# Turning the gated rows of both SwiGLU layers by transposing DMAs in 16-bit halves, in place of TensorE transposes

## The chip, the core and the metric

The kernel runs on one core of a Trainium2 chip. The core has TensorE (PE: matmuls, and in the profile PEld for the loads of the stationary operand), VectorE (DVE), ScalarE (ACT), GpSimd (POOL) and SyncE (SP), which here only issues DMAs. Each engine runs its own instructions in order and they meet at semaphores. SBUF is the memory on the chip (128 partitions), PSUM the eight banks that TensorE writes into, and 16 DMA engines move data. The metric is the device time of one execution in microseconds. Differences are told as time, and as a ratio where two kernels are compared.

## The reference

One decoder layer on 256 tokens of width 2048, all in float32:

```python
h = x
h = h + 0.5 * swiglu(rmsnorm(h, g_ffn1), w1_gate, w1_up, w1_down)      # f1
z = rmsnorm(h, g_mix) @ w_in
y = concat(rmsnorm(spatial_gating(...)), rmsnorm(window_attention_sinks(...)))
h = h + y @ w_out
h = h + cross_attention(rmsnorm(h, g_x), rmsnorm(mem, g_mem), w_xq, w_xkv, w_xo)
h = h + 0.5 * swiglu(rmsnorm(h, g_ffn2), w2_gate, w2_up, w2_down)      # f2
return rmsnorm(h, g_final)

def swiglu(x, w_gate, w_up, w_down):       # w_gate, w_up: 2048 x 5632, w_down: 5632 x 2048
    return (silu(x @ w_gate) * (x @ w_up)) @ w_down
```

The change touches the product silu(gate) * up of both SwiGLUs: a matrix of 256 tokens x 5632 columns that the next matmul contracts over its 5632 columns.

## The kernel before

**Products.** Every float32 operand is split into a high part that TensorE's fast 32-bit format (fp32r) holds exactly and a low part, the rest; a product takes three matmuls (high x high, low x high, high x low). `split` (L145 to L147) makes the two: ScalarE casts the high part (L146), VectorE subtracts it from the source for the low part (L147). Weights come as chunks of 1 MB, a tile of 128 x 4 x 512, and `load` issues their DMA on SP (L317 and L340) and splits them. Three raw chunks fit (tag raw, 3 buffers), and two of the split ones (tags wh and wl).

**Chunk kinds.** A chunk stands for a 2x2 block product. An N or C chunk takes 24 matmuls of 128x128 by 512 columns (four products of two terms); an S chunk takes 21, a seven-product form, and needs sums of weight blocks: VectorE makes them (tile t: L319, L322, L323), and they are split too (th and tl). The sums have one buffer each, so one S chunk's sums must be used up before the next one's take their place. An S chunk saves TensorE three matmuls and costs VectorE more.

**The gate/up stage of a SwiGLU.** `ffn` runs 11 units (index c, 0 to 10), each of eight chunks, for 512 columns of gate and the same 512 of up. Units 2 to 9 have four S chunks, the others three, and the first unit of f1 has none. When a unit's products are complete, `seven_early` and `seven_late` (L560 to L571) put them together from PSUM on VectorE, `gated` applies Silu on ScalarE (L671) and multiplies on VectorE (L675 in f1, L677 in f2), once for each half of the tokens (tb, 0 and 1). The result is two tiles of 128 tokens x 512 columns (`rows_`; in the profile f1gp and f1gz, f2gp and f2gz; f1sg in f1's first unit).

**The turn.** The down stage contracts over columns, so columns must lie on partitions. `rows_done(c, rows_)` does it: it takes an SBUF tile `a` (m4, 128 x 1024), and queues a generator `work` as side work. For each q (0 and 1) it calls `transposed` (L230), which does four 128x128 transposes on TensorE into one PSUM bank, two blocks of columns by two halves of the tokens, in the order that the kind of the down chunk wants (`laid`). ScalarE copies the bank to `a` (L665). `acts[2 * c + q]` is then set, and later `inner` fills the forms that the down stage multiplies.

**What sets the order.** TensorE's instructions run in program order. The other engines' order, SP's included, is laid out by a planner when the kernel is built: it simulates the program with its own estimates of durations, and takes what is ready by priority, earlier in the program first. `turn` keeps one chunk's matmuls pending: it writes the loads and splits of a chunk into the program, then the matmuls of the chunk before with its follow-up work (`post`, at high priority), and then those entries of the list `later` whose count has come to 0; each turn takes one off the counts. Side work is taken up during the matmuls, a step after every six (`side_step`), and a generator's `yield 5` asks for five steps of pause, `yield 2` for two. Thus the transposes of a unit's rows stand among the matmuls of the next unit's second and third chunks, or for the last unit among those of the first down chunks.

**Buffers.** Tag s2 has six buffers of 128 x 512 float32; it holds the parts of a unit while they are put together, the gated rows among them, and small intermediates. Tag tr has four PSUM banks, three of which the seven-product form uses.

Of the kernel before, what the change touches and what calls it, by code (L numbers as in the profile page):

```python
# [7 lines left out]

F32 = mybir.dt.float32
F32R = mybir.dt.float32r  # L10
AF = mybir.ActivationFunctionType
ALU = mybir.AluOpType
AX = mybir.AxisListType

P = 128
T = 256
TB = 2
# [15 lines left out]
def layer_kernel(  # L33
# [22 lines left out]
    nc = tc.nc  # L56
# [13 lines left out]
    def nm(s):  # L70
        uid[0] += 1
        return f"{s}_{uid[0]}"

    def m4(s):
        return mid.tile([P, 1024], F32, tag="m4", name=nm(s))

    def s2(s):
        return tmp.tile([P, 512], F32, tag="s2", name=nm(s))

    def bank(s):  # L80
        return trp.tile([P, 512], F32, tag="tr", name=nm(s))
# [8 lines left out]
    def silu_table():  # L90
        t = tiny.tile([P, 1], F32, tag="warmed", name=nm("warmed"))
        return nc.scalar.activation(t, ones[:, :1], AF.Silu)

# [24 lines left out]
    h = const.tile([P, TB, D], F32, name="h")  # L118
# [15 lines left out]
    def square_into(parts_ap, src, width):  # L134
        junk = s2("junk")
        nc.scalar.activation(junk[:, :width], src, AF.Square, accum_out=parts_ap)

    def split_scaled(hi, lo, src, g):

        nc.scalar.activation(hi, src, AF.Copy, scale=g)  # L140
        nc.vector.scalar_tensor_tensor(
# [27 lines left out]
    def form(s):  # L169
        return [fp.tile([P, 4, P], F32R, tag=t, name=nm(s + t)) for t in ("fh", "fl")]  # L170

    class Pair:
        def __init__(self, s, kind, base=None):
            self.kind = kind
            self.base = base or form(s)
            if kind in "SD":
                self.sums = form(s)
                if kind == "D":
                    self.more = [
                        const.tile([P, 2, P], F32R, tag="more" + t, name=nm(s + "more")) for t in "hl"  # L180
                    ]
# [40 lines left out]
    def laid(kind, k, tb):  # L222
        return BASE[kind].index(f"A{tb + 1}{k + 1}")

    def transposed(s, kind, src):

        ps = bank(s).rearrange("p (k t) -> p k t", k=4)
        for k in range(2):
            for tb in range(TB):
                nc.tensor.transpose(ps[:, laid(kind, k, tb), :], src(tb, k), ident)  # L230
        return ps

    def row_tile(kind, v, k):

        return v[:, k::2, :] if kind == "C" else v[:, 2 * k:2 * k + 2, :]

    def pair_from_rows(s, kind, src, gcol):
# [4 lines left out]
        for k in range(2):  # L242
# [4 lines left out]
            else:  # L247
                nc.scalar.activation(row_tile(kind, raw, k), row_tile(kind, ps, k), AF.Copy, scale=g)
        if kind != "N":
# [60 lines left out]
    def load(s, w, kind, pieces, between):  # L310

        raw = stream.tile([P, 4, 512], F32, tag="raw", name=nm(s + "w"), bufs=3)
        wh = stream.tile([P, 4, 512], F32R, tag="wh", name=nm(s + "wh"))
        wl = stream.tile([P, 4, 512], F32R, tag="wl", name=nm(s + "wl"))
        b = {name: (wh[:, i, :], wl[:, i, :]) for name, i in SLOT.items()}
        if kind == "S":
# [9 lines left out]
            for i, names in enumerate((("T1", "T3"), ("T2", "T4"))):  # L326
                th, tl = [
                    stream.tile([P, 2, 512], F32R, tag=f"{n}{i}", name=nm(s + n), bufs=1)
                    for n in ("th", "tl")
# [93 lines left out]
    def side_add(gen):  # L423
        side.append([now[0], gen])
# [33 lines left out]
    later = []  # L458
# [55 lines left out]
    def narrow_unit(s, w, pairs, late, beside):  # L514

        ps = []
        for c in range(2):
            raw = stream.tile([P, 8, 256], F32, tag="raw", name=nm(s + "w"), bufs=3)
            wh = stream.tile([P, 8, 256], F32R, tag="wh", name=nm(s + "wh"))
            wl = stream.tile([P, 8, 256], F32R, tag="wl", name=nm(s + "wl"))  # L520
# [33 lines left out]
    KINDS_D = "NNSNSNSN" + "NSNSNSN" + "NNSNSNN"  # L554
# [41 lines left out]
    def adds(s, c, j0, on_block=None):  # L596
# [10 lines left out]
        def early(u):  # L607
            p1, v, z = s2(s + "p1"), s2(s + "v"), s2(s + "z")
            nc.scalar.activation(p1, u["P1"], AF.Copy, scale=c)
            nc.vector.scalar_tensor_tensor(  # L610
# [40 lines left out]
    def ffn(s, get, rs, wgu, wd, on_block, first=None, on_token_block=None):  # L651
        acts = [None] * 22
        pairs = [None] * 22

        def rows_done(c, rows_):
            a = m4(s + "a").rearrange("p (q k t) -> p q k t", q=2, k=4)

            def work():
                for q in range(2):
                    yield 5 if q == 0 else 2  # L660
                    ps = transposed(
                        s + "a", KINDS_D[2 * c + q],
                        lambda tb, k: rows_[tb][:, (2 * q + k) * P:(2 * q + k + 1) * P],
                    )
                    nc.scalar.copy(a[:, q], ps)  # L665
                    acts[2 * c + q] = a[:, q]

            side_add(work())

        def gated(up, sg, r, tb):  # L670
            nc.scalar.activation(  # L671
                sg[1], sg[0], AF.Silu, scale=1.0 if r is None else r[:, tb:tb + 1]
            )
# [13 lines left out]
        def gu_unit(c):  # L687
            got = {}

            def late(u):  # L690
                r = rs()
                c22 = s2(s + "u")
                at = {(0, 0): got["p1"], (1, 1): c22, (0, 1): got["v"], (1, 0): got["z"]}
                seven_late(u, got, lambda tb, j: at[tb, j])
                gated(at[0, 1], (at[0, 0], at[0, 0]), r, 0)
                gated(c22, (at[1, 0], at[1, 0]), r, 1)
                rows_done(c, (at[0, 0], at[1, 0]))

            kinds = MORE if 2 <= c <= 9 else FEWER
            order = range(8)  # L700
            if c == (first is not None):
                order = ORDER[first is None]
            u = Unit(s + "g", "".join(kinds[j] for j in order))
            for i in range(8):
                push(
                    u, i, wgu[order[i], c], lambda j=order[i]: get(j),
                    lambda i=i: (
                        i == u.kinds.rindex("S") and seven_early(u, got), i == 7 and late(u)
                    ),
                    beside=lambda i: (  # L710
                        first[2](8 + i) if first is not None and c == 1
                        else rs() if (c, i) == (0, 5) else inner(i - 5) if c == 10 and i >= 5 else None
                    ),
                )

        def plain_gu_unit(c):
            pairs_, before, prep, rs0 = first
            u = Unit(s + "g", "N" * 8, alone=(7,))
            u.gate_first = True

            def late():
                r = rs0()
                sg = [s2(s + "sg") for _ in range(TB)]
                for tb, (g, up) in enumerate((("P2", "Q3"), ("Q4", "R"))):
                    gated(u[up], (u[g], sg[tb]), r, tb)
                rows_done(c, sg)

            pieces = {0: (1, 0, 3, 2), 1: (1, 3, 0, 2)}
            for i in range(8):
                push(  # L730
                    u, i, wgu[i, c], lambda i=i: have(pairs_, i), late if i == 7 else None,
                    pieces=pieces.get(i), beside=prep, before=before,
                )
# [747 lines left out]
```

## Time and profile before

| | |
|---|---|
| median of 3 runs | 2049.84 us (2049.66 to 2049.85) |
| span of the profiled execution (first to last instruction) | 2047.2 us |
| its own time, beside the span | not listed apart; the runs' median lies 2.6 us above the span |
| TensorE busy | 2034.8 us (99%) |
| VectorE busy | 1859.5 us (91%) |
| ScalarE busy | 1225.4 us (60%) |
| DMA engines | 402.21 MB, SP's queue 53.0% of 16 engines' span |
| TensorE clock granted | 0.999 of full speed |

Times are from one execution. A row of a group gives the line, engine, operation, what is written <- what is read with the shapes, how often, and durations; a row of the timeline gives the start and the length in microseconds, and in brackets how long the engine was idle before it and what ended that. Matmuls overlap, so the starts of neighbours tell what one costs, not its length. A wait row names who waited and for whom, with the total, the number and the longest.

### The profile page before, as it was taken

The page shows a single profiled execution, that of the slowest core. Times are in us where ns is not written, and L with a number is a line of the kernel's source. Part 1 is how long each engine was busy: PE and PEld are TensorE (multiplying, and loading weights), DVE is VectorE, ACT ScalarE, POOL GpSimd, SP SyncE. Part 2 cuts the span into 40 slices and gives each one's busy share as a digit, 9 for nine tenths or more (in the row PEclk, how much of TensorE's full clock was granted, in tenths as well). Part 3 has the DMA queues.
Part 4 walks back from the last instruction along what each step waited for, and adds up shares of the span by engine and source line. Part 5 has one row for each costly group of instructions (what it writes and reads, how often), then busy time and mean ns, then how long its engine had stood idle before and what let it go on. Part 6 is the DMA issues. An engine that isn't in the chain of part 4 may idle for free.

```text
span 2047.2 us, 24505 instructions
## 1 busy us (share of the span) xinstructions
PE 2034.8 (99%) x9411; PEld 1690.0 (83%) x9411; DVE 1859.5 (91%) x1998; ACT 1225.4 (60%) x1344; POOL 36.6 (2%) x57
## 2 busy tenths in 40 slices
PE   9999999999999999999999999999999999999998
PEld 7888888888888888888888888888888888888886
DVE  6999999999998978988988977899999999999988
ACT  7755555565555766655556665675555556565554
POOL 0000000000000110100000000000000000000000
PEclk9999999999999999999999999999999999999999
DMA  8555555555555565545545544455455555555563
GB/s 312 182 207 204 206 206 185 205 209 192 203 204 203 188 241 178 195 162 185 202 169 186 204 150 155 171 195 214 185 206 202 205 193 206 202 203 209 185 224 126
DMA packets 60421, 402.21 MB, mean 196 GB/s; under 512 B 6912, under 2 KB 8976, under 8 KB 13200
## 3 DMA queue, kind: packets, MB, share of 16 engines
q1 hardware_dynamic: 57856, 393.50, 53.0%
q0 software_dynamic: 2016, 6.30, 0.9%
q8 instruction: 74, 1.21, 0.2%
q10 hardware_dynamic: 432, 0.84, 0.1%
q14 instruction: 43, 0.35, 0.1%
HBM read 398.52 MB, written 2.10 MB: 196 GB/s over the span
## 4 chain that ended last, share of the span: by engine, by line
PE 97%; DVE 1%; ACT 1%; issue 0%; DMA 0%; POOL 0%; POOLq 0%; DVEq 0%; SPq 0%
PE f1gQ L410 16%; PE f2gQ L410 15%; PE f2dQ L410 6%; PE f1dQ L410 6%; PE f1gP L410 6%; PE f2gP L410 6%; PE xqQ L410 3%; PE f2dP L410 3%; PE f1dP L410 3%; PE woQ L410 2%; PE xoQ L410 2%; PE f2dR L410 2%; PE f1dR L410 2%; PE vQ L410 2%; PE mv0Q L410 2%; PE mv1Q L410 2%
## 5 line engine op out<-in xcount | busy, mean ns | idle before, releaser
L147 DVE TENSOR_TENSOR f1gwl<-f1gw,f1gwh 128x1536 fp32r<-128x1536 f32 (+2 forms) x94 | 181.7, 1935 | 19.8 <-ACT f1gwh L146 16.0
L146 ACT CAST f2gwh<-f2gw 128x1536 fp32r<-128x1536 f32 (+1 forms) x88 | 150.7, 1712 | 69.0 <-PE f2gQ L410 45.5
L146 ACT CAST f1gwh<-f1gw 128x1536 fp32r<-128x1536 f32 (+2 forms) x94 | 153.0, 1629 | 59.9 <-PE f1gQ L410 39.0
L147 DVE TENSOR_TENSOR f2gwl<-f2gw,f2gwh 128x1536 fp32r<-128x1536 f32 (+1 forms) x88 | 179.4, 2039 | 9.5 <-ACT f2gwh L146 7.8
L146 ACT CAST f2gth<-f2gt 128x1024 fp32r<-128x1024 f32 x82 | 84.9, 1050 | 75.9 <-DVE f2gt L319 28.8
L146 ACT CAST f1gth<-f1gt 128x1024 fp32r<-128x1024 f32 x76 | 79.0, 1051 | 76.1 <-DVE f1gt L319 30.1
L410 PE MATMUL f2gQ<-f2gwh,n4fh 128*128 128x512 f32 x317 | 124.5, 393 | 0.0
L410 PE MATMUL f2gQ<-f2gwh,n4fl 128*128 128x512 f32 x317 | 123.4, 389 | 0.0
L146 ACT CAST f2dwh<-f2dw 128x2048 fp32r<-128x2048 f32 (+1 forms) x44 | 77.3, 1757 | 61.6 <-PE f2dQ L410 39.6
L410 PE MATMUL f1gQ<-f1gwh,n1fh 128*128 128x512 f32 x286 | 112.4, 393 | 0.0
L410 PE MATMUL f1gQ<-f1gwh,n1fl 128*128 128x512 f32 x286 | 111.3, 389 | 0.0
L146 ACT CAST f1dwh<-f1dw 128x2048 fp32r<-128x2048 f32 (+1 forms) x44 | 77.3, 1758 | 56.6 <-PE f1dQ L410 38.1
L147 DVE TENSOR_TENSOR f2gtl<-f2gt,f2gth 128x1024 fp32r<-128x1024 f32 x82 | 99.6, 1220 | 8.9 <-ACT f2gth L146 8.4
L147 DVE TENSOR_TENSOR f1dwl<-f1dw,f1dwh 128x2048 fp32r<-128x2048 f32 (+1 forms) x44 | 92.1, 2093 | 12.6 <-ACT f1dwh L146 12.5
L147 DVE TENSOR_TENSOR f2dwl<-f2dw,f2dwh 128x2048 fp32r<-128x2048 f32 (+1 forms) x44 | 92.1, 2094 | 11.5 <-ACT f2dwh L146 11.3
L147 DVE TENSOR_TENSOR f1gtl<-f1gt,f1gth 128x1024 fp32r<-128x1024 f32 x76 | 92.4, 1220 | 7.7 <-ACT f1gth L146 7.2
L410 PE MATMUL f2gQ<-f2gwl,n4fh 128*128 128x512 f32 x317 | 97.6, 392 | 0.0
L410 PE MATMUL f1gQ<-f1gwl,n1fh 128*128 128x512 f32 x286 | 88.0, 393 | 0.0
L410 PEld LDWEIGHTS f2gQ<-f2gwh,n4fh 128*128 128x128 f32 x317 | 59.5, 188 | 12.3 <-DVE f2gv L569 0.4
L410 PEld LDWEIGHTS f2gQ<-f2gwh,n4fl 128*128 128x128 f32 x317 | 59.5, 188 | 11.9
L410 PE MATMUL f2gP<-f2gwh,n4fh 128*128 128x512 f32 x176 | 68.8, 391 | 0.0
L410 PEld LDWEIGHTS f2gQ<-f2gwl,n4fh 128*128 128x128 f32 x317 | 58.8, 188 | 12.0
(828 smaller groups left out, 6045.8 us busy)
## 6 DMA issues: line engine op xcount, KB each, us to landing
f2gw<-in_w_gu SPq DMA_DIRECT2D x88, 1024.0 KB, 4.8
f1gw<-in_w_gu SPq DMA_DIRECT2D x86, 1024.0 KB, 4.9
f1dw<-in_w_down SPq DMA_DIRECT2D x44, 1024.0 KB, 4.8
f2dw<-in_w_down SPq DMA_DIRECT2D x44, 1024.0 KB, 4.8
wow<-in_w_out SPq DMA_DIRECT2D x16, 1024.0 KB, 4.8
xqw<-in_w_xq SPq DMA_DIRECT2D x16, 1024.0 KB, 4.8
xow<-in_w_xo SPq DMA_DIRECT2D x16, 1024.0 KB, 4.8
qw<-in_w_in SPq DMA_DIRECT2D x8, 1024.0 KB, 4.8
```

Of the source, the lines that this page charges most:

```text
L146: nc.scalar.copy(hi, src)
L147: nc.vector.tensor_tensor(lo, src, hi.bitcast(F32), ALU.subtract)
L410: nc.tensor.matmul(self.banks[name], x, y, start=name not in self.begun, stop=self.left[name] == 0)
```

## The change

`rows_done` no longer uses TensorE, nor PSUM. A DMA transposes 16-bit elements, so the 32-bit rows are taken as pairs of 16-bit words:

- `turned`, in the turn in which the rows are gated: for each half of the tokens ScalarE copies the row tile (128 tokens x 512 float32, seen as 1024 words of 16 bits) into an s2 tile `w`, the 512 low halves first and the 512 high halves behind them. Then a transposing DMA on SP's queue turns `w` into another s2 tile `t`: eight blocks of 128x128 words, four of the low halves and four of the high ones, each with columns on partitions.
- `joined`, two turns later: for each q and each half of the tokens a ScalarE copy takes two blocks of low and of high halves from `t` and writes them interleaved into `a`, so that 32-bit numbers stand there again, at the places that `laid` gives. Then `acts` is set as before.

Both go through the list `later`, not through the side work. Per unit that is two parting copies of 128x1024 words, two transposing DMAs of 256 KB, and four joining copies of 128x512 words, in place of eight transposes and two copies of 128x512 from PSUM.

```diff
         def rows_done(c, rows_):
-            a = m4(s + "a").rearrange("p (q k t) -> p q k t", q=2, k=4)
-
-            def work():
+            a = m4(s + "a")
+            words = a.bitcast(U16).rearrange("p (q i t h) -> p q i t h", q=2, i=4, h=2)
+            halves_ = []
+
+            def turned():
+                for tb in range(TB):
+                    w = s2(s + "w").bitcast(U16)
+                    nc.scalar.copy(
+                        w.rearrange("p (h c) -> p h c", h=2),
+                        rows_[tb].bitcast(U16).rearrange("p (c h) -> p h c", h=2),
+                    )
+                    t = s2(s + "t").bitcast(U16)
+                    nc.sync.dma_start_transpose(t.rearrange("p (b r) -> p b r", b=8), w)
+                    halves_.append(t.rearrange("p (h b t) -> p b t h", h=2, b=4))
+
+            def joined():
                 for q in range(2):
-                    yield 5 if q == 0 else 2
-                    ps = transposed(
-                        s + "a", KINDS_D[2 * c + q],
-                        lambda tb, k: rows_[tb][:, (2 * q + k) * P:(2 * q + k + 1) * P],
+                    kind = KINDS_D[2 * c + q]
+                    for tb in range(TB):
+                        i, j = laid(kind, 0, tb), laid(kind, 1, tb)
+                        nc.scalar.copy(
+                            words[:, q, i:j + 1:j - i], halves_[tb][:, 2 * q:2 * q + 2]
+                        )
+                    acts[2 * c + q] = a[:, q * 512:(q + 1) * 512].rearrange(
+                        "p (k t) -> p k t", k=4
                     )
-                    nc.scalar.copy(a[:, q], ps)
-                    acts[2 * c + q] = a[:, q]
-
-            side_add(work())
+
+            later.append((0, turned))
+            later.append((2, joined))
```

`U16` is the 16-bit unsigned type.

More of the change, by code (lines that the diff above doesn't have):

```diff
@@ L10 @@
 F32R = mybir.dt.float32r
+U16 = mybir.dt.uint16
 AF = mybir.ActivationFunctionType
```

## The prediction

> **What bounds the kernel now.** I read the page first (busy times, the chain that ended last), then what TensorE waited for, then the stretch of one gate/up unit in order of time.
>
> ```profile
> span 2047.2 us, 24505 instructions
> PE 2034.8 (99%) x9411; PEld 1690.0 (83%) x9411; DVE 1859.5 (91%) x1998; ACT 1225.4 (60%) x1344; POOL 36.6 (2%) x57
> PE 97%; DVE 1%; ACT 1%; issue 0%; DMA 0%; POOL 0%; POOLq 0%; DVEq 0%; SPq 0%
> ...
> PE xoQ L410 <- ACT n4r L248: 1.2, 1, 1.2
> ```
>
> TensorE is the chain: 97% of it, and the longest of its waits is 1.2 us, once. Whatever leaves TensorE's in-order queue shortens the span, as long as the engines that feed it keep up. The page alone doesn't say whether they do; the stretches of one unit each do (columns: length, then busy us of PE, PEld, DVE, ACT, POOL, granted clock, DMA share, GB/s):
>
> ```profile
> 231.45:273.23 41.78, 41.78 (x192) 34.58 (x190) 40.05 (x38) 24.13 (x22) 0.00 (x0) 1.00 0.55 202
> 1566.66:1608.43 41.77, 41.77 (x192) 34.57 (x190) 40.15 (x38) 24.05 (x22) 0.00 (x0) 1.00 0.54 202
> 52.00:95.00 43.00, 43.00 (x207) 35.57 (x206) 42.81 (x54) 33.16 (x45) 0.00 (x0) 1.00 0.52 186
> ```
>
> In a unit with four S chunks TensorE needs all of 41.77 us and VectorE 40.05 to 40.15 of them; in FFN 1's second unit VectorE is busy 42.81 of 43.00. VectorE is a second bound about 1.6 us behind the first. ScalarE has 17.6 us to spare in a unit, and the DMA engines are half idle.
>
> **What is removed.** The transposes at L230, four in a group, and the two ScalarE copies behind them. The same eight weight matmuls with a group among them and without one (TensorE in order of time; start, length):
>
> ```profile
> 147.07 0.62 PE L410 MATMUL f1gP<-f1gwl,n1fh 128*128 128x512 f32 x2
> 147.53 0.27 PE L230 MATMUL f1a<-ident,f1gp 128*128 128x128 f32 x1
> ...
> 147.89 1.64 PE L410 MATMUL f1gQ<-f1gwl,n1fh 128*128 128x512 f32 x6
> 149.36 0.39 PE L410 MATMUL f1gP<-f1gwh,n1fh 128*128 128x512 f32 x1
> ...
> 158.27 0.61 PE L410 MATMUL f1gP<-f1gwl,n1fh 128*128 128x512 f32 x2
> 158.72 1.52 PE L410 MATMUL f1gQ<-f1gwl,n1fh 128*128 128x512 f32 x6
> 160.08 0.39 PE L410 MATMUL f1gP<-f1gwh,n1fh 128*128 128x512 f32 x1
> ```
>
> 149.36 - 147.07 = 2.29 us against 160.08 - 158.27 = 1.81 us: a group costs 0.48 us, not the 4 x 0.27 that its rows show, because matmuls overlap. The copies tell how many groups there are:
>
> ```profile
> L665 ACT COPY f1a<-f1a x22: 572/584/590, 64.6 to 485.6; 128x512 f32<-128x512 f32 x22
> L665 ACT COPY f2a<-f2a x22: 577/587/590, 1398.1 to 1820.8; 128x512 f32<-128x512 f32 x22
> ```
>
> 44 groups x 0.48 = **21.1 us off TensorE**, 0.96 in each of 22 units. That is the most this change can bring: nothing else is taken from the chain. ScalarE loses 2 x 0.58 = 1.2 us per unit.
>
> **What is added on ScalarE.** Per unit two copies that part the halves (128x1024, 16 bit) and four that join them (128x512). No row has a 16-bit operand; the nearest are the casts of as many elements:
>
> ```profile
> L146 ACT CAST f1gth<-f1gt x76: 1040/1052/1078, 53.0 to 457.6; 128x1024 fp32r<-128x1024 f32 x76
> L146 ACT CAST f1afh<-f1a x22: 610/618/632, 393.6 to 630.0; 128x512 fp32r<-128x512 f32 x22
> ```
>
> 2 x 1.05 + 4 x 0.62 = 4.6 us. From below, half of that if a 16-bit element took half the time; from above, double if a stride of two halved the rate. I take 4.6, since time here goes with the number of elements. Net 3.4 us per unit, 75 us in all, against 17.6 idle per unit: no bound by its sum. What counts is where they stand, since ScalarE runs in order and its casts feed VectorE. The places, in one unit of FFN 1 (ScalarE, VectorE, SP's issues, then TensorE):
>
> ```profile
> 270.73 1.05 ACT L146 CAST f1gth<-f1gt 128x1024 fp32r<-128x1024 f32 x1 [2.87 <-DVE f1gt L319]
> 272.66 1.91 ACT L146 CAST f1gwh<-f1gw 128x2048 fp32r<-128x2048 f32 x1 [0.87 <-PE f1gQ L410]
> 274.47 0.58 ACT L665 COPY f1a<-f1a 128x512 f32<-128x512 f32 x1
> 274.95 1.06 ACT L146 CAST f1gth<-f1gt 128x1024 fp32r<-128x1024 f32 x1
> 276.71 0.59 ACT L665 COPY f1a<-f1a 128x512 f32<-128x512 f32 x1 [0.70 <-PE f1a L230]
> 277.22 1.49 ACT L146 CAST f1gwh<-f1gw 128x1536 fp32r<-128x1536 f32 x1
> 284.71 1.91 ACT L146 CAST f1gwh<-f1gw 128x2048 fp32r<-128x2048 f32 x1
> ...
> 268.80 0.68 DVE L675 TENSOR_TENSOR f1gz<-f1u,f1gz 128x512 f32<-128x512 f32 x1
> 272.81 1.22 DVE L147 TENSOR_TENSOR f1gtl<-f1gt,f1gth 128x1024 fp32r<-128x1024 f32 x1
> 277.16 1.22 DVE L147 TENSOR_TENSOR f1gtl<-f1gt,f1gth 128x1024 fp32r<-128x1024 f32 x1
> 278.41 1.23 DVE L319 TENSOR_TENSOR f1gt<-f1gw 128x1024 f32<-128x1024 f32 x1
> 279.55 1.75 DVE L147 TENSOR_TENSOR f1gwl<-f1gw,f1gwh 128x1536 fp32r<-128x1536 f32 x1
> 284.85 1.23 DVE L147 TENSOR_TENSOR f1gtl<-f1gt,f1gth 128x1024 fp32r<-128x1024 f32 x1 [1.20 <-ACT f1gth L146]
> ...
> 268.31 0.33 SPq L317 DMA_DIRECT2D f1gw<-in_w_gu  x1
> 274.69 0.33 SPq L340 DMA_DIRECT2D f1gw<-in_w_gu  x1
> ...
> 279.05 1.07 PE L410 MATMUL f1gQ<-f1gtl,n1fh 128*128 128x512 f32 x4
> ```
>
> The second gated row is done at 269.48 and the first 0.6 earlier; ScalarE is idle from about 267.9 to 270.73. The parting copies take 268.9 to 271.0, push the cast at 270.73 by 0.3, and its reader on VectorE (272.81) has 1.0 to spare: nothing. Without that idle stretch they would cost 2.1 us of ScalarE ahead of a cast. The four joining copies fall where the two old ones stood, around 274.5 to 279, and are 2.5 - 1.2 = 1.3 us longer. The tight place is the cast at 274.95: its low half ends at 278.4, and TensorE reads the last of those four operands from about 279.5, 1.1 us later, and 0.96 less than that once the transposes are gone. Between 0 (they fill the idle time, and the cast goes ahead) and 1.3 us per unit (all of it ahead of a cast) I take 0.2, near the low end, since the first joining copy replaces an equal old one: 22 x 0.2 = **+4.4 us**.
>
> **What is added on SP and the DMA engines.** 44 transfers of 256 KB from SBUF to SBUF. No row transposes in a DMA; by size the nearest are (KB each, median us to landing):
>
> ```profile
> f1gw<-in_w_gu SPq DMA_DIRECT2D x86, 1024.0 KB, 4.9
> mTr<-in_memT POOLq DMA_DIRECT2D x16, 128.0 KB, 3.3
> n0r<-in_xT SPq DMA_DIRECT2D x7, 256.0 KB, 7.2
> out<-hg SPq DMA_DIRECT2D x1, 256.0 KB, 3.9
> sm<-in_small ACTq DMA_DIRECT2D x1, 52.0 KB, 2.5
> ```
>
> So 2.5 us (the smallest transfer) to 7.2 (the same size, queued among other loads). I take 4 to 5: 3.9 for the size, plus part of the load that SP issued at 268.31 and that moves until about 273. Issued at about 270.0 and 271.3, the pair lands by about 276. As bytes they are 11.5 MB beside 402 MB on engines that are busy 55% of the time: nothing. On SP a transfer waits for its parting copy and the next weight load waits behind it; that load is issued at 274.69, so the pair may hold the queue for 3 us before anything shifts, and its tile is first read at 284.71, 5 us after it lands. Were that cover gone, each us of delay would pass to TensorE. Lifetimes: the six s2 buffers hold the two rows and four more while the pair is under way, and two were free; the PSUM bank becomes free, which nothing waits for.
>
> **VectorE as the next bound.** TensorE now needs 41.77 - 0.96 = 40.81 us a unit, VectorE 40.05 to 40.15: only 0.7 us may stay idle, where 1.7 are idle today. A part is waiting for buffers that TensorE frees and shrinks by itself. The 1.20 at 284.85 is another kind: VectorE waits for a cast of what it has itself just made. At worst it stays whole and a unit takes 40.05 + 1.20 = 41.25; at best it goes, 40.81. I take the middle, 0.22 lost in each of 17 such units (eight in each FFN, and the second of FFN 1): **+3.7 us**.
>
> **The sum.** -21.1 + 4.4 + 3.7 = -13.0 us on a span of 2047.2. The median of the runs, 2049.84, lies 2.6 above the span, and I leave that as it is: **2036.8 us**. My own bounds for the forecast are 2028.7 (all 21.1) and 2041.
>
> **Rivals.** (1) *VectorE takes over*: the 17 full units keep 41.77 us because VectorE can't lose its idle time, and only the other five gain 0.96: 2049.8 - 4.8 = 2045. For it: 42.81 of 43.00. Against: TensorE never waits for VectorE today. Chance 0.20.
>
> (2) *Slower: ScalarE stands at the joining copies.* They are in order ahead of the cast at 277.22, whose reader on VectorE starts at 279.55. The cast must start by 278.06, three joining copies (1.85 us) before it, so the second transfer must land by 276.2, 4.9 us after its issue; from 5.6 on VectorE's spare 0.7 us is used up too, and from 6.6 the gain of 0.96 is gone. At 7.2 us (the row of that size) ScalarE starts the cast at 280.3, VectorE waits until 281.8, 2.25 us late, 1.55 beyond its spare: 42.36 us a unit, 22 x 0.6 = +13, 2063. For it: ScalarE's place in the order is laid out by a planner's estimate of the landing, and the true one is unknown. Against: loads four times the size land in 4.9. Chance 0.25.
>
> (3) *The turning goes block by block*, each of a transfer's eight 128x128 blocks paying a small transfer's landing: 8 x 2.5 = 20 us, 40 for the pair, so that ScalarE stands some 33 us in each unit: 22 x 33 = +726, about 2775. For it: nothing in this trace; against: a plain 1 MB load lands in 4.9 as one stream. Chance 0.07. The Trainium skill, "VectorE: DVE Perf Modes", section "The three transpose paths", speaks for it: it gives 1309 ns for one 128x128 bf16 block by DMA against 390 on TensorE. By that figure a transfer would be an estimated 10.5 us and the time an estimated 2,400; this trace has TensorE's side far lower (0.48 us for a group of four, in 32 bits), so the page's own comparison would be worse still for DMA. "DMA: Bandwidth & Descriptors", section "Latency and other measured facts", has 261 GB/s for such transfers, which would be an estimated 1 us each and agrees with the forecast; no run here shows either yet.
>
> **Chances and range.** Forecast 0.48, rivals 0.20, 0.25, 0.07. A difference under 0.2%, 4.1 us, can't be told from none: rival 1 straddles that edge (a little over half of it faster), and a small part of rival 2 lies within it. Faster 0.59, same 0.12, slower 0.29. The range runs from 2028 to 2063, which leaves out rival 3 and the worse half of rival 2.
>
> **What would show it.** Right: no L230 row on f1a and f2a, units of 40.8 to 41.1 us, the transposing DMAs landing in under 5 us, VectorE over 97% busy in a unit. Rival 1: units of 41.7 with TensorE waiting for low halves. Rival 2: ScalarE idle at the joining copies, put down to the transposing DMA, and TensorE waiting behind it. Rival 3: those DMAs landing in 10 us or more.

## The result, and the profile after

The changed kernel takes 2054.82 us (median; 2053.67 to 2056.67) beside 2049.76 us for the kernel before on the same chip: a ratio of 1.0027 (95% interval 1.0017 to 1.0036), 5.1 us slower, just past the 0.2% that can be told from no change. The forecast was 2036.8, 13.0 us faster. So the sign was wrong, though the time lies in the stated range, whose upper end came from rival 2 with a transfer of 7.2 us.

The page of the changed kernel (span, busy times, the chain that ended last by engine):

```profile
span 2051.8 us, 24290 instructions
...
PE 2021.7 (99%) x9235; PEld 1672.0 (81%) x9235; DVE 1859.9 (91%) x1998; ACT 1293.0 (63%) x1432; POOL 34.4 (2%) x57
...
PE 85%; DVE 5%; ACT 5%; DMA 3%; issue 2%; SPq 0%; POOL 0%; POOLq 0%; DVEq 0%; ACTq 0%
```

The 9411 - 9235 = 176 transposes are gone. But TensorE is 85% of the chain where it was 97%: ScalarE, VectorE and the DMA are on it now. TensorE's two longest entries in the view of waits (total us, times, longest), and ScalarE's for the transposing DMA, are new:

```profile
PE f1gQ L411 <- ACT f1gth L147: 8.7, 8, 2.4
PE f1gQ L411 <- DVE f1gtl L148: 6.9, 8, 0.9
...
ACT f1a L677 <- DMA f1t<-f1w: 20.1, 9, 3.8
ACT f2a L677 <- DMA f2t<-f2w: 10.2, 10, 1.2
```

(In this kernel the casts are at L147, the low halves at L148, the parting copies at L664, the transposing DMAs at L669, the joining copies at L677.) TensorE's two waits are in FFN 1, though ScalarE stands for the DMA in both FFNs. Where the time went is told by one VectorE row that each unit but FFN 1's first has once, `f1u` or `f2u`: from its first start to its last lie nine units of FFN 1 and ten of FFN 2. Before, then after:

```profile
L568 DVE TENSOR_TENSOR f1u<-f1gQ,f1gz x10: 680/684/686, 95.2 to 472.7; 128x512 f32<-128x512 f32 x10
L568 DVE TENSOR_TENSOR f2u<-f2gQ,f2gz x11: 684/684/686, 1388.5 to 1807.9; 128x512 f32<-128x512 f32 x11
```

```profile
L569 DVE TENSOR_TENSOR f1u<-f1gQ,f1gz x10: 681/683/685, 96.8 to 485.8; 128x512 f32<-128x512 f32 x10
L569 DVE TENSOR_TENSOR f2u<-f2gQ,f2gz x11: 683/684/686, 1400.8 to 1813.2; 128x512 f32<-128x512 f32 x11
```

FFN 1 takes 389.0 us between these starts where it took 377.5 (+11.5, and 1.6 more ahead of the first). FFN 2 takes 412.4 where it took 419.4 (-7.0). What lies between and behind them is 1.5 shorter. Together +4.6, which is 2051.8 - 2047.2. So the same change lost in one FFN and won in the other. One full unit of each, in the windows view (columns as in the prediction):

```profile
271.13:314.33 43.20, 41.38 (x181) 33.63 (x181) 40.13 (x39) 27.16 (x25) 0.00 (x0) 1.00 0.62 207
1607.41:1648.38 40.97, 40.97 (x182) 33.71 (x181) 40.16 (x38) 27.42 (x25) 0.00 (x0) 1.00 0.62 218
```

Both were 41.77. FFN 2 has nearly the forecast's best unit (40.81), with TensorE busy throughout. In FFN 1 TensorE is idle 1.8 of 43.20 us. The place, in order of time (start, length; ScalarE first, then VectorE, SP, TensorE):

```profile
275.59 1.04 ACT L664 COPY f1w<-f1gp 128x1024 uint16<-128x1024 uint16 x1
276.53 1.05 ACT L664 COPY f1w<-f1gz 128x1024 uint16<-128x1024 uint16 x1
279.92 0.68 ACT L677 COPY f1a<-f1t 128x512 uint16<-128x512 uint16 x1 [2.34 <-DMA f1t<-f1w]
280.50 1.05 ACT L147 CAST f1gth<-f1gt 128x1024 fp32r<-128x1024 f32 x1
281.46 1.85 ACT L677 COPY f1a<-f1t 128x512 uint16<-128x512 uint16 x3
283.22 1.90 ACT L147 CAST f1gwh<-f1gw 128x2048 fp32r<-128x2048 f32 x1
285.03 1.03 ACT L147 CAST f1gth<-f1gt 128x1024 fp32r<-128x1024 f32 x1
...
278.06 1.22 DVE L320 TENSOR_TENSOR f1gt<-f1gw 128x1024 f32<-128x1024 f32 x1
282.73 0.69 DVE L324 TENSOR_TENSOR f1gt<-f1gt,f1gw 128x512 f32<-128x512 f32 x1
285.15 2.29 DVE L148 TENSOR_TENSOR f1gwl<-f1gw,f1gwh 128x2048 fp32r<-128x2048 f32 x1 [1.73 <-ACT f1gwh L147]
...
276.66 2.62 SPq L669 DMA_TRANSPOSE f1t<-f1w  x2
...
286.11 0.50 PE L411 MATMUL f1gQ<-f1gth,n1fh 128*128 128x512 f32 x1 [0.95 <-ACT f1gth L147]
288.63 0.73 PE L411 MATMUL f1gQ<-f1gtl,n1fh 128*128 128x512 f32 x2 [0.87 <-DVE f1gtl L148]
```

The first joining copy stands directly behind the two parting copies. ScalarE is done with those at 277.58, and the transfer issued at 276.66 lands at about 279.9, so it stands 2.34 us. Behind it in order is the first cast of the sums: they are ready at 279.28 (L320), the cast starts 1.2 late. Three joining copies more and a cast of 1.90 stand ahead of the second: ready at 283.42 (L324), started at 285.03, 1.6 late. VectorE waits 1.73 for the cast of 1.90, the weights' cast, which came behind the three copies. TensorE, with its queue shortened by the transposes, then waits 0.95 us for the second cast of the sums, and 0.87 more for its low half, which VectorE makes behind the late weights.

In FFN 2 the order on ScalarE is another:

```profile
1611.84 1.04 ACT L664 COPY f2w<-f2gp 128x1024 uint16<-128x1024 uint16 x1
1612.79 1.05 ACT L147 CAST f2gth<-f2gt 128x1024 fp32r<-128x1024 f32 x1
1613.74 1.04 ACT L664 COPY f2w<-f2gz 128x1024 uint16<-128x1024 uint16 x1
1615.97 1.26 ACT L677 COPY f2a<-f2t 128x512 uint16<-128x512 uint16 x2 [1.19 <-DMA f2t<-f2w]
1617.14 1.91 ACT L147 CAST f2gwh<-f2gw 128x2048 fp32r<-128x2048 f32 x1
1618.95 1.04 ACT L147 CAST f2gth<-f2gt 128x1024 fp32r<-128x1024 f32 x1
...
1612.91 1.23 SPq L669 DMA_TRANSPOSE f2t<-f2w  x1
1614.58 0.33 SPq L318 DMA_DIRECT2D f2gw<-in_w_gu  x1
1614.96 1.23 SPq L669 DMA_TRANSPOSE f2t<-f2w  x1
```

Here the first cast goes between the parting copies, ahead of the stand, the stand is half as long, and two copies instead of four lie between it and the second cast.

The transfers themselves, in the views of the tiles (minimum, median and maximum of what one holds SP, in ns; then from issue to landing in us), FFN 1 and then the landing in FFN 2:

```profile
L669 SPq DMA_TRANSPOSE f1t<-f1w x22: 1232/1280/1523, 52.0 to 491.9; - x22
...
DMA to landing us min/median/max: 3.0/3.2/4.7
```

```profile
DMA to landing us min/median/max: 3.0/3.2/6.9
```

### The profile page after: what moved, and what is told of

It reads as the page before. It is cut to its first block, busy times and chain, and to the rows that moved or that the text cites. A ratio compares the mean times of both kernels' runs of the same rounds, so it can differ in the third digit from the quotient of the medians.

```text
span 2051.8 us, 24290 instructions
## 1 busy us (share of the span) xinstructions
PE 2021.7 (99%) x9235; PEld 1672.0 (81%) x9235; DVE 1859.9 (91%) x1998; ACT 1293.0 (63%) x1432; POOL 34.4 (2%) x57
## 4 chain that ended last, share of the span: by engine, by line
PE 85%; DVE 5%; ACT 5%; DMA 3%; issue 2%; SPq 0%; POOL 0%; POOLq 0%; DVEq 0%; ACTq 0%
PE f2gQ L411 14%; PE f1gQ L411 11%; PE f2dQ L411 6%; PE f1dQ L411 5%; PE f2gP L411 5%; PE f1gP L411 4%; PE xqQ L411 3%; PE f2dP L411 3%; PE f1dP L411 2%; PE woQ L411 2%; PE xoQ L411 2%; PE f2dR L411 2%; ACT f1gwh L147 2%; PE vQ L411 2%; PE mv0Q L411 2%
## 5 line engine op out<-in xcount | busy, mean ns | idle before, releaser
L148 DVE TENSOR_TENSOR f1gwl<-f1gw,f1gwh 128x1536 fp32r<-128x1536 f32 (+2 forms) x94 | 181.8, 1935 | 37.6 <-ACT f1gwh L147 37.0
L148 DVE TENSOR_TENSOR f2gwl<-f2gw,f2gwh 128x1536 fp32r<-128x1536 f32 (+1 forms) x88 | 179.2, 2038 | 8.1 <-ACT f2gwh L147 7.5
L147 ACT CAST f2gwh<-f2gw 128x1536 fp32r<-128x1536 f32 (+1 forms) x88 | 150.6, 1711 | 48.9 <-PE f2gQ L411 32.6
L147 ACT CAST f1gwh<-f1gw 128x1536 fp32r<-128x1536 f32 (+2 forms) x94 | 153.0, 1628 | 40.8 <-PE f1gQ L411 14.7
L147 ACT CAST f1gth<-f1gt 128x1024 fp32r<-128x1024 f32 x76 | 79.7, 1051 | 90.4 <-DVE f1gt L320 59.0
L147 ACT CAST f2gth<-f2gt 128x1024 fp32r<-128x1024 f32 x82 | 85.2, 1049 | 56.0 <-DVE f2gt L324 30.7
L147 ACT CAST f2dwh<-f2dw 128x2048 fp32r<-128x2048 f32 (+1 forms) x44 | 77.3, 1758 | 58.5 <-PE f2dQ L411 37.3
L147 ACT CAST f1dwh<-f1dw 128x2048 fp32r<-128x2048 f32 (+1 forms) x44 | 77.2, 1757 | 49.0 <-PE f1dQ L411 31.6
L148 DVE TENSOR_TENSOR f1dwl<-f1dw,f1dwh 128x2048 fp32r<-128x2048 f32 (+1 forms) x44 | 92.0, 2093 | 10.1 <-ACT f1dwh L147 10.0
L148 DVE TENSOR_TENSOR f2dwl<-f2dw,f2dwh 128x2048 fp32r<-128x2048 f32 (+1 forms) x44 | 92.1, 2093 | 10.0 <-ACT f2dwh L147 9.9
L148 DVE TENSOR_TENSOR f2gtl<-f2gt,f2gth 128x1024 fp32r<-128x1024 f32 x82 | 99.8, 1220 | 1.0
L148 DVE TENSOR_TENSOR f1gtl<-f1gt,f1gth 128x1024 fp32r<-128x1024 f32 x76 | 92.5, 1219 | 2.3 <-ACT f1gth L147 1.7
L411 PE MATMUL f1gQ<-f1gth,n1fh 128*128 128x512 f32 x152 | 60.1, 395 | 8.7 <-ACT f1gth L147 8.7
```

The costliest lines, as they stand in the source:

```text
L147: nc.scalar.copy(hi, src)
L148: nc.vector.tensor_tensor(lo, src, hi.bitcast(F32), ALU.subtract)
L411: nc.tensor.matmul(self.banks[name], x, y, start=name not in self.begun, stop=self.left[name] == 0)
```

## The experiments

My theory after the result: the whole loss is ScalarE's stand at the first joining copy in FFN 1, with what is queued behind it. The rivals: the transfers disturb the weight loads; the 3.4 us more of ScalarE work per unit push the casts by themselves; VectorE doesn't keep up with the shorter units. "Units" below is the usual time from one `f1u` (or `f2u`) start to the next in the full units: 41.77 before in both FFNs, after 43.15 and 41.0. (FFN 1's first full unit is longer: 42.7 before, 44.9 after.)

**The turn left out.** Against the kernel before; ScalarE copies the untransposed rows where it copied the bank, so the result's turn is left out, and with it TensorE's transposes, the DMAs and the 16-bit copies.

```diff
-                    ps = transposed(
-                        s + "a", KINDS_D[2 * c + q],
-                        lambda tb, k: rows_[tb][:, (2 * q + k) * P:(2 * q + k + 1) * P],
+                    nc.scalar.copy(
+                        a[:, q], rows_[q].rearrange("p (k t) -> p k t", k=4)
                     )
-                    nc.scalar.copy(a[:, q], ps)
```

> This is the kernel before without the 44 groups of TensorE transposes; ScalarE copies the gated rows to the tile unturned, so the turn is left out of the computation. It shows what TensorE can gain at most. Theory (a group costs 0.48 us and VectorE can follow): gate/up units of 40.8 us in both FFNs and 2028.7 us in all, 21 under the kernel before. Rival (VectorE becomes the bound at 41.25 us a unit, the 1.20 us wait for its own cast staying whole): 2028.7 + 17 x 0.44 = 2036.

2032.98 us, ratio 0.9922 (0.9907 to 0.9937), 16.0 faster: between the two expectations. In FFN 2 the units are about 40.8, in FFN 1 they are not:

```profile
235.90:277.13 41.23, 41.09 (x181) 33.70 (x180) 39.93 (x38) 24.20 (x21) 0.00 (x0) 1.00 0.56 203
```

41.25 is the figure that the prediction had as VectorE's worst. So without any turn about 5 us of the 21.1 can't be had. The rows show VectorE at the bound: its one listed wait in this unit is 1.06 us, for a weights' cast, and TensorE comes late once a unit, at a low half of the sums (VectorE, then TensorE at the start of the next unit):

```profile
242.83 2.29 DVE L147 TENSOR_TENSOR f1gwl<-f1gw,f1gwh 128x2048 fp32r<-128x2048 f32 x1 [1.06 <-ACT f1gwh L146]
277.67 0.73 PE L410 MATMUL f1gQ<-f1gtl,n1fh 128*128 128x512 f32 x2 [0.15 <-DVE f1gtl L147]
```

The first of these two matmuls starts 0.54 us after the one before it and the second 0.34 after the first, where neighbours stand 0.23 apart: 0.42 lost, about the difference of the units. Whether less work on VectorE removes it is tested by the last experiment.

**The change in FFN 2 alone, and in FFN 1 alone.** Both versions of `rows_done` are kept, and one line picks by stage (`"f1"` in the second kernel):

```diff
+        rows_done = rows_turned_by_dma if s == "f2" else rows_turned_by_pe
```

> FFN 2 is turned by DMA as in the changed kernel, FFN 1 on TensorE as before. In the changed kernel FFN 1 takes 12.3 us more than before (its place at the first FFN 2 unit) and FFN 2 7.7 less. Theory (the loss lies in FFN 1's ScalarE order alone): 2049.8 - 7.7 = 2042 us, units of FFN 2 at 40.9 to 41.0. Rival (the DMA turn costs everywhere and FFN 2 gained only since FFN 1 ran late): 2048 to 2052.

> FFN 1 is turned by DMA as in the changed kernel, FFN 2 on TensorE as before. Theory (the loss is FFN 1's alone): 2049 + 12.3 = 2061 us, units of 43.1 in FFN 1 and of 41.8 in FFN 2. Rival (the two FFNs' effects are not apart): 2052 to 2057.

FFN 2 alone: 2042.59 us, ratio 0.9967 (0.9954 to 0.9980), 6.3 faster, with units of 41.0 there. FFN 1 alone: 2062.29 us, 1.0061 (1.0046 to 1.0076), 12.6 slower, with units of 43.15 there. The loss and the gain each keep to their own stage, and add up to what the changed kernel shows (12.6 - 6.3 = 6.3 beside 5.1), within the intervals.

**The joining copies held behind the casts.** The changed kernel with one edge more in ScalarE's order: the joining copies come after the cast that stands last in the program when they are written. All work is kept.

```diff
+    last_cast = [None]
...
-        nc.scalar.copy(hi, src)
+        last_cast[0] = nc.scalar.copy(hi, src)
...
             def joined():
+                with tc.issue_after(last_cast[0].ins):
+                    join()
+
+            def join():
                 for q in range(2):
```

> The changed kernel, the joining copies held behind the last cast of the chunk that is written ahead of them, so that in FFN 1 both casts of the sums go before the joining copies. Work and transfers are the same. Theory (in FFN 1 the first joining copy waits 2.3 us for its transfer ahead of a cast, and three more stand ahead of the next): the 2.1 us that TensorE waits in each of eight or nine FFN 1 units go, units of 40.9 to 41.3, about 2034 to 2037 us in all. Rival (ScalarE's 3.4 us more work a unit costs wherever it stands): within 3 us of the changed kernel, 2052 to 2057.

2035.29 us, ratio 0.9931 (0.9917 to 0.9946), 13.6 faster than before and as expected; no other kernel here that computes the whole layer is as fast. ScalarE in order of time in FFN 1 (the casts are at L149 here, the joining copies at L683; the second parting copy ends at 269.1), and one unit in the windows view:

```profile
270.88 1.05 ACT L149 CAST f1gth<-f1gt 128x1024 fp32r<-128x1024 f32 x1 [1.81 <-DVE f1gt L322]
271.98 1.92 ACT L149 CAST f1gwh<-f1gw 128x2048 fp32r<-128x2048 f32 x1
274.81 1.05 ACT L149 CAST f1gth<-f1gt 128x1024 fp32r<-128x1024 f32 x1 [0.91 <-DVE f1gt L326]
275.77 2.43 ACT L683 COPY f1a<-f1t 128x512 uint16<-128x512 uint16 x4
```

```profile
262.62:303.89 41.27, 41.12 (x181) 33.71 (x181) 39.95 (x39) 27.28 (x25) 0.00 (x0) 1.00 0.65 218
```

ScalarE now waits for VectorE's sums and not for the DMA: the four joining copies run without a stand, because the second transfer landed at 272.6, about 3 us before the first of them. With the same transfers and the same ScalarE work per unit (27.28 us beside 27.16) this order is 2.3 us over the kernel without a turn, and 18.7 better than the changed kernel (each taken against the kernel before). So neither disturbed loads nor ScalarE's amount of work made the loss. The edit moves all four copies, though: whether the stand or the copies ahead of the casts cost the time, the next two runs tell apart.

**The stand taken away, the copies still ahead of the casts.** The joining copies read the parted tile instead of the transposed one, so nobody reads what the DMA brings; the 16-bit blocks stay unturned.

```diff
-                    halves_.append(t.rearrange("p (h b t) -> p b t h", h=2, b=4))
+                    halves_.append(w.rearrange("p (h b t) -> p b t h", h=2, b=4))
```

> The changed kernel, but the joining copies read the parted tile and not the turned one, so they wait for no transfer; the transfers still run, and the turn is left out of the result. Here the planner puts all four joining copies ahead of the first cast in FFN 1 and ahead of the next high part in FFN 2. If the standing wait for the landing (2.34 us a unit) is all of the loss: FFN 1 units of 40.8 to 41.0, about 2034 us. If the place of the copies counts beside the wait: the first cast comes 0.4 us earlier and the second 1.6, FFN 1 units of 41.4 to 41.9, about 2040 to 2044. If it is ScalarE's work as such: 2052 to 2057.

2033.87 us, ratio 0.9926 (0.9910 to 0.9943). ScalarE in order of time, in FFN 1:

```profile
267.57 0.68 ACT L677 COPY f1a<-f1w 128x512 uint16<-128x512 uint16 x1
...
269.11 1.85 ACT L677 COPY f1a<-f1w 128x512 uint16<-128x512 uint16 x3
270.86 1.05 ACT L147 CAST f1gth<-f1gt 128x1024 fp32r<-128x1024 f32 x1
```

The order is not quite that of the changed kernel: all four joining copies are ahead of the first cast, where three of them came behind it. Even so the units of FFN 1 are 41.24. So without the stand neither the copies' length nor their place ahead of the casts costs anything. Against its kernel before this one is 15.1 faster and the changed one 5.1 slower, so taking the wait away is worth 20 us, and FFN 1 has 17.6 of them (371.4 us from the first `f1u` start to the last, 389.0 in the changed kernel). The DMAs still run here: beside the kernel without a turn, they and the added ScalarE work come to 0.9 us together, too little to be told from none.

**The joining copies two turns later.** A count in the list `later`:

```diff
-            later.append((2, joined))
+            later.append((4, joined))
```

> The changed kernel, the joining copies put into the program four turns later and not two. In FFN 1 the planner still lays the first joining copy ahead of the first cast of the sums, so that ScalarE will still stand there for the landing; the other three now come after the next high part. Theory (the stand for the landing comes first, and what is laid between it and the next casts adds to it): the stand stays at 2.0 to 2.4 us a unit, the next high part comes 1.8 us earlier than in the changed kernel, FFN 1 units of 41.4 to 42.4, about 2040 to 2047 us. If the stand alone makes the loss, whatever follows it: 43 us a unit and 2052 to 2057. If more program distance were what is needed: 2033 to 2036.

2040.92 us, ratio 0.9959 (0.9944 to 0.9974), with units of 41.45 in FFN 1. The stand is the same (in the view of waits again 20.1 us over 9 times, 3.8 at the longest), only what is queued behind it differs (ScalarE in order of time):

```profile
274.33 0.69 ACT L677 COPY f1a<-f1t 128x512 uint16<-128x512 uint16 x1 [2.32 <-DMA f1t<-f1w]
274.93 1.05 ACT L147 CAST f1gth<-f1gt 128x1024 fp32r<-128x1024 f32 x1
275.88 1.91 ACT L147 CAST f1gwh<-f1gw 128x2048 fp32r<-128x2048 f32 x1
277.68 1.26 ACT L677 COPY f1a<-f1t 128x512 uint16<-128x512 uint16 x2
278.85 1.04 ACT L147 CAST f1gth<-f1gt 128x1024 fp32r<-128x1024 f32 x1
```

From the end of the stand to the second cast it is 278.85 - 274.33 = 4.5 us, where the changed kernel has 285.03 - 279.92 = 5.1. The weights' cast comes 275.88 - 274.33 = 1.55 us after it, against 283.22 - 279.92 = 3.30. These 0.6 and 1.75 us are what differs on ScalarE between units of 43.15 and of 41.45. So a stand of 2.3 us costs 0.2 us a unit by itself (41.45 beside 41.24), and the other 1.7 come from the copies that stand between it and the weights' cast; the loss needs both. A longer stand does cost by itself: in FFN 1's first full unit it is 3.8 us, and this unit stays at 44.7 us, 44.9 in the changed kernel and 41.3 where nothing waits for the landing. The run also shows that the count in `later` doesn't set where the first copy stands: only the other three moved.

**The joining copies on GpSimd.** GpSimd is idle in these stages, so the stand would hold up nobody:

```diff
-                        nc.scalar.copy(
+                        nc.gpsimd.tensor_copy(
```

> The changed kernel with the four joining copies on GpSimd, which is busy 2% of the time and has nothing else in order there, so that it can stand for the landing and nobody waits behind it. Theory: as without any turn, FFN 1 units of 41.2 to 41.3, 2033 to 2036 us. Rival (GpSimd's traffic slows VectorE, which has 0.3 us a unit to spare): VectorE's operations longer than before and units over 41.6, 2038 to 2050.

My theory's number was missed: 2053.45 us, ratio 1.0018 (1.0008 to 1.0027). The units are 41.75 and 41.9, and the first `f1u` starts at 101.0, 5.8 us later than in the kernel before. One unit in the windows view with the page, the tile view of the sums' low halves, and VectorE in order of time beside such a copy:

```profile
143.12:184.88 41.76, 41.29 (x182) 33.63 (x181) 41.52 (x39) 25.03 (x21) 13.90 (x4) 1.00 0.63 214
PE 2025.2 (99%) x9235; PEld 1672.6 (81%) x9235; DVE 1893.9 (92%) x1998; ACT 1244.4 (61%) x1344; POOL 287.0 (14%) x145
```

```profile
L148 DVE TENSOR_TENSOR f1gtl<-f1gt,f1gth x76: 1209/1219/1698, 56.3 to 467.3; 128x1024 fp32r<-128x1024 f32 x76
```

```profile
287.79 1.04 DVE L324 TENSOR_TENSOR f1gt<-f1gt,f1gw 128x512 f32<-128x512 f32 x1
```

ScalarE is rid of 49 us, but VectorE is busy 34 us more for the same 1998 instructions: single subtractions take up to 1.70 us instead of 1.22, and the sum at L324 1.04 instead of 0.69. With VectorE 0.7 us per unit from being the bound, 34 us over 22 units (1.5 each) take the gain away: VectorE is now busy 41.52 of a unit's 41.76 us. The rival of this expectation had the mechanism, with more loss than it said. GpSimd pays too: its shortest joining copy takes 0.66 us, the median one 1.7, and four of a unit 13.9. The Trainium skill, "SBUF — State Buffer", section "SBUF: two separate sides", has a rule of that kind: VectorE and GpSimd share a pair of ports as an exclusive lock, and a VectorE instruction with two operands in SBUF meets it against a GpSimd instruction that reads SBUF. The rows agree in which instructions grow: 84 VectorE instructions, each with two operands in SBUF, are 0.29 to 0.48 us longer, and ScalarE's casts beside the same copies keep their time to 0.02 us. That the lock is the cause was not tested apart.

**The held order, and fewer sums on VectorE.** To see whether VectorE is what keeps FFN 1 at 41.25: the held order again, with one of a chunk's sums left out (the fourth), a neighbouring part split in its place.

```diff
-            nc.vector.tensor_tensor(t[:, 3, :], t[:, 2, :], raw[:, 3, :], ALU.add)
...
-                split(th, tl, t[:, 2 * i:2 * i + 2, :])
+                split(th, tl, t[:, i:i + 2, :])
```

> The joining copies held behind the casts as in the run that does this, and VectorE's fourth sum of weight blocks left out of every S chunk in all stages (the low products take a sum twice instead, so this part of the computation is missing). It takes four operations of 0.6 us from VectorE in each full unit and nothing from TensorE. Theory (the 41.25 us that FFN 1's units keep even without a turn are VectorE's, 0.44 over TensorE's 40.81): units of 40.8 in both FFNs, about 2031 us. Rival (the 0.44 has another cause, a load or ScalarE): 41.2 stays, 2034 to 2036.

2028.24 us, ratio 0.9895 (0.9881 to 0.9910): the units came as expected, the time 3 us lower. The planner laid ScalarE's copies out differently here: in most full units of FFN 1 two joining copies, behind one cast of the sums and ahead of the weights' cast, stand 1.0 us for the landing. The starts of the units:

```profile
L570 DVE TENSOR_TENSOR f1u<-f1gQ,f1gz x10: 684/684/686, 97.3 to 465.1; 128x512 f32<-128x512 f32 x10
L570 DVE TENSOR_TENSOR f2u<-f2gQ,f2gz x11: 684/684/686, 1379.7 to 1789.0; 128x512 f32<-128x512 f32 x11
```

Now the span from the first to the last is 367.8 us in FFN 1 (389.0 in the changed kernel) and 409.3 in FFN 2 (412.4): full units of 40.80 in both, and the gain is 21.4 us. A full unit is 0.97 us shorter than before, where the two groups of transposes in it were put at 0.96: with the transfers, the parting, the joining and a stand all still there, a unit gains the whole of what left TensorE. That the total comes so near to 21.1 is partly chance. VectorE is busy 81 us less in all (1778.5), which helped where it had been close to the bound (FFN 1's first full unit went from 42.7 to 40.7), and the first `f1u` starts 2.1 us later. What the fewer sums alone are worth in the kernel before was not run.

| kernel | us | against before | full units FFN 1 / FFN 2 |
|---|---|---|---|
| changed | 2054.82 | +5.1 | 43.15 / 41.0 |
| in FFN 1 alone | 2062.29 | +12.6 | 43.15 / 41.77 |
| in FFN 2 alone | 2042.59 | -6.3 | 41.77 / 41.0 |
| joined on GpSimd | 2053.45 | +3.8 | 41.75 / 41.9 |
| joined two turns later | 2040.92 | -8.8 | 41.45 / 41.0 |
| joined behind the casts | 2035.29 | -13.6 | 41.27 / 40.8 |
| no wait for the landing | 2033.87 | -15.1 | 41.24 / 40.9 |
| no turn at all | 2032.98 | -16.0 | 41.25 / 40.8 |
| behind the casts, fewer sums | 2028.24 | -21.4 | 40.80 / 40.80 |

## Why the prediction was wrong, step by step

- **What leaves TensorE (-21.1): right.** 0.97 us a full unit measured once nothing else bounds, 0.96 forecast.
- **The parting copies (nothing): right.** ScalarE is done with them at 277.58 in the unit quoted, 1.7 us before the sums are ready.
- **The joining copies (+4.4, "The four joining copies fall where the two old ones stood"): the step that failed.** The first of them does not replace an old copy at the old copy's place. In FFN 1 it is laid directly behind the parting copies, ahead of the first cast of the sums, and ScalarE stands there. I priced the copies by their own length, 0 to 1.3 us a unit, and the wait of the first one at nothing. The length alone costs nothing (units of 41.24 with all four ahead of the cast and no wait); the stand, with three copies between it and the weights' cast, costs 1.9 us in a full unit of FFN 1, and taking it away is worth 20 us in all. The old copies waited too, but for TensorE's transposes, which stood late in the order (276.71 in the unit before); the new ones wait for a DMA that starts as soon as the rows are gated.
- **The landing (4 to 5 us): too long, and it didn't help.** 3.2 us. (The 2.5 us that the prediction gives to the smallest transfer are the 52 KB row's; a smaller one, 8 KB, has 4.5, so those rows don't go by size.) Rival 2 made 4.9 us after the issue the point from which a stand decides, reckoned from the cast at 277.22 in the unit quoted, the old place. At the new place every landing over some 0.9 us makes ScalarE stand (issued at 276.66, ScalarE done with the second parting copy at 277.58). So the rival had the mechanism and the sign, but by the same error of place it asked for a slow transfer, where a fast one was enough. Its condition spoke for a chance of 0.25; with the place left open it should have had more.
- **VectorE as the next bound (+3.7, 40.81 to 41.25): right in its bounds, split by stage, by another wait.** FFN 1 goes to the upper end, 41.25, FFN 2 stays near the lower, 40.8 to 41.0. Without a turn it comes to 21.1 - 16.0 = 5.1 us. The wait that stays is 1.06 us for a weights' cast, not the 1.20 for the cast of the sums, so that 41.25 was hit is partly luck. Rival 1 (units stay at 41.77) is out.
- **ScalarE's amount (4.6 us added): near.** Parting 1.04 us (1.05 taken), joining 0.68 (0.62 taken): 4.8.
- **SP and the weight loads (nothing): right.** SP is held some 1.2 to 1.3 us per transfer (once 2.9), and with transfers and copies all there the kernel without the wait is within 0.9 us of the one without a turn.
- **Rival 3 (block by block) is out**: eight blocks land in 3.2 us. The 1309 ns per block of the Trainium skill, "VectorE: DVE Perf Modes", section "The three transpose paths", doesn't add up over a transfer; with a fixed part in it, it isn't contradicted for a single block. Of the 261 GB/s of "DMA: Bandwidth & Descriptors", section "Latency and other measured facts", these runs say little: at 1 us for 256 KB, by that figure an estimate, some 2 of the 3.2 would be fixed, and no run has another size.
- **The sum.** -13.0 forecast; with the copies behind the casts, near the order that the forecast had in mind, the kernel gave -13.6. That the two agree is partly luck, since the parts are differently shared: 5.1 for VectorE, about 2.4 for the rest. The changed kernel does the same work in another order: one joining copy ahead of both casts of the sums, three ahead of the weights' cast.

What stays open: why the planner lays the first joining copy ahead of the cast in FFN 1 and behind it in FFN 2. The two stages differ on VectorE even where nothing is turned (41.25 against 40.8), so the sums become ready at another moment, but that this sets the choice, and which landing the planner reckons with, was not shown.

## What to carry to other kernels

When work moves to a DMA, the transfer's own price matters less than where its reader stands: on an engine that runs in order, a wait costs by what is queued behind it, and the same 2.3 us stand cost 1.9 us a unit in one order and 0.2 in another. Ask of each new reader what will be next to it in the order, not next to the instruction it replaces, and hold it behind the work that the bound engine waits for. A stage that is built by the same code may be laid out differently elsewhere, so read a unit of each, after the change as before it.

## What the hardware showed unexpectedly

- In eight of FFN 2's eleven pairs a 1 MB weight load was issued on SP's queue between the two transfers (the SP rows quoted above). The second transfer then took 6.2 to 6.9 us to land, where FFN 2's pairs without a load between took 3.0 to 3.2 each. It cost nothing there, because the copies that need it stand late: in the last run, where FFN 2 has such loads too (6.0 us and more to land), its units are 40.80.
- A joining copy of 512 16-bit elements with an interleaved read and write takes 0.68 us, longer than the cast of 512 32-bit ones (0.62); the parting copy, 1024 16-bit elements, takes 1.04, no less than a 32-bit cast of 1024. Half the bytes saved no time on ScalarE.
- With the joining copies on GpSimd, 84 of VectorE's instructions with two SBUF operands were 0.29 to 0.48 us longer, and the copies themselves took 0.66 to 13.9 us. ScalarE's casts beside them were not longer.
